# A two-layer decoder trunk: the mixer's gate projection in front of its key projection, and tile 1's output gate made by hand

## The chip, the cores and the metric

The kernel runs on one core of one Trainium2 chip. Its time is the device time of one execution in microseconds (us); lower is better. The engines are TensorE (PE, matrix products), VectorE (DVE), ScalarE (ACT), GpSimd (POOL) and SyncE (SP, which issues the transfers of the weights).

## The reference, cut to what matters

There are 256 tokens of width 1024 and two layers. Each layer is a half-step SwiGLU FFN, a token mixer and a second half-step FFN, each followed by a layer norm. The mixer is what the change touches:

```
h = x @ w_in                 # one projection, its columns split into groups
(nq, kc, vc, ks, vs, kw, vw, gl, u, gq, gk, gv, ga, gr) = split(h)
gates = sigmoid(gl)                                   # for the attention's three branches
o_a = nsa_mixer(nq, kc, vc, ks, vs, kw, vw, gates)    # compressed / selected / window attention
o_b = pool_mixer(u)                                   # trailing means
# gated linear attention:
log_a = log_sigmoid(ga @ wa2 + ba) / 16               # low-rank forget gate
b = cumsum(log_a) in chunks of 64;  q_t = gq * exp(b);  k_t = gk * exp(-b)
o_c = rmsnorm(gla(q_t, k_t, gv)) * norm_g * silu(gr)  # silu(gr) is the output gate
out = concat(o_a, o_b, o_c) @ w_out
```

In `nsa_mixer` the raw keys and values `kc`, `vc` are gathered into blocks of 32 positions, `pe` is added, and the blocks go through `gelu(flat @ w1) @ w2`: this is called the compression below.

## The kernel before, in words

**Tiles.** The 256 tokens are two tiles of 128, t = 0 and 1. The activations `x` are transposed on TensorE and kept as a high and a low part (`xh`, `xl`). A large matmul is three products of such parts (`mm3`): high by high, high by low, low by high.

**Weights.** A weight half (128x1024, or 128x592 for the gate chunk) is loaded by SP into one of four `raw` buffers. ACT copies its high part into `wh` (L236), VectorE makes the low part `wl = raw - wh` (L238); there are eight buffers of each. Both tiles use the same halves. The list `units` sets the order in which halves are loaded and split: FFN, then the mixer's projection in the order `WIN_ORDER`, four halves for each chunk, then the output projection, then the next FFN.

**The mixer's steps.** `ORDER` (L47) is the program order of the mixer, a letter for the step and a digit for the tile: `k` is `chunk_keys`, `g` `chunk_gates`, `f` `gates`, `q` `chunk_queries`, `c` `compress`, `v` `chunk_values`, `a` one step of the attention, `r` `chunk_rest` (the last chunk), `s` the load of ACT's silu table, `p` the pooling, `l` the end of the linear attention, `w` a step of the output projection. A scheduler then places instructions on the engines by priority along this order, as their inputs and buffers come, so the end of the FFN and its layer norm interleave with the first steps of the mixer. Each engine runs its instructions in the order so fixed.

- `chunk_keys` projects the keys and values. ACT copies them out of PSUM (`c0`, four key pieces; `kv`, the raw keys and values of the compression). TensorE transposes `c0`; ACT and VectorE make `ksh` and `ksl` of it. TensorE transposes `kv` into a bank of the kind `acc`; VectorE copies it with four `zr` copies and adds `pe` twice (`zA`, `zB`), 128x256 each.
- `chunk_gates` projects the gates. ACT copies `c3` (the attention's gates and the low-rank gate) and makes the silu of `gr` in `grs`. TensorE transposes `c3`, VectorE copies `gaT` (L604), TensorE multiplies it by `wa2` (L606), and ACT and VectorE begin the log-sigmoid (`az`, `mn`).
- `gates` loads ACT's table of exponential and logarithm (once, for tile 0), finishes the log-sigmoid, makes the cumulative sums `bc` by two scans and three exponentials of them (`eb`, `enb`, `ekh`), and `eg`, one plus an exponential of the attention's gates.
- `compress` needs `zA` and `zB` of both tiles: 32 matmuls on them (L676), a gelu on VectorE and ACT over the small tile `tg`, its copy `grep` (L691), and the product with `w2` (L694).
- `chunk_queries` copies the queries, transposes them, and keeps a high part on ACT (L762) and a correction on VectorE (L763), both in `qs`.
- `chunk_rest` projects the last chunk into `c4`, and GpSimd multiplies `grs` by `norm_g` (L772). That multiply is placed as soon as `grs` is there.
- The softmax of the attention is made by VectorE (scores with mask into `P`, L811) and ACT (exponential, L813); TensorE then transposes `P`.

PSUM has single banks `g0`, `g1`, `tr0`, `tr1`, and two banks each for `acc0` and `acc1`.

Of the kernel before, what the change touches and what calls it, by code (L numbers as in the profile page):

```python
# [10 lines left out]
def _warn_once_fixed(msg, *args, **kwargs):  # L11
# [11 lines left out]
AF = mybir.ActivationFunctionType  # L23
ALU = mybir.AluOpType
# [18 lines left out]

LAST = (10, 8, 9)
WARM = ((7, 512), (4, 128))
WIN_ORDER = (0, 3, 1, 2, 4)
ORDER = ("k0 g0 k1 g1 f0 f1 q0 c v0 a0 a0 a0 a0 q1 v1 a0 r1 a0 a1 a1 r0 a1 a1 a1 a1 a1 a1 a1 a1 s "  # L47
         "p0 l0 w0 w0 w0 p1 w0 w1 l1 w1 w0 w1 w1 w1")
TAGS = {
    "b2": (("c0", "c1", "qm"), 4),  # L50
    "b1": (("zr", "sq", "pl", "c2", "kv"), 3),
    "b05": (("c3", "az", "mn", "gaT", "qt", "kt", "kq"), 6),
    "P": (("P",), 4),
}
# [2 lines left out]
def build(ctx, tc, d):  # L57
    nc = tc.nc
    PE, ACT, DVE, POOL = nc.tensor, nc.scalar, nc.vector, nc.gpsimd
# [57 lines left out]
    for t in range(2):  # L117
        vbd.append(cst.tile([128, 2, 2, 64], F32, name=f"vbd{t}"))
        a = cst.tile([128, 4, 128], F32, name=f"at{t}")
# [57 lines left out]
    for l in range(L):  # L177
        def ffn_units(f):
            def down(c):
                if c >= 0:  # L180
                    halves([d["wd"][l, f, (2 * c + h) * 128:(2 * c + h + 1) * 128, :] for h in range(2)], 1024)

            for c, q in ((0, 0), (1, 0), (0, 1), (1, 1)) if (l, f) == (0, 0) else ((0, 0), (0, 1), (1, 0), (1, 1)):
                halves(gate_up(l, f, c, q), 1024)
            for x in PLAN:
                if x[0] == "S":
                    fs = seven(l, f, int(x[1:]))
                elif x[0] in "ab":
                    halves(gate_up(l, f, int(x[1:]), "ab".index(x[0])), 1024)
                elif x[0] == "d":  # L190
                    down(int(x[1:]))
                elif x[0] != "T":
                    units.append(fs[x])
            for c in LAST:
                down(c)
        ffn_units(0)
        for c in WIN_ORDER:
            for q in range(2):
# [92 lines left out]
    def bank(kind, t):  # L291

        return psum.tile([128, 512], F32, name=f"{kind}{t}", bufs=2 if kind == "acc" else 1)

    def transposes(t, srcs, kind="tr"):
        p = bank(kind, t)
        for i, s in enumerate(srcs):
            pe(PE.transpose(p[:, i * 128:(i + 1) * 128], s, ident))  # L298
        return p
# [274 lines left out]
    def mt(t, name, shape, dt=F32):  # L574
        for tag, (names, n) in TAGS.items():
            if name in names:
                return mix.tile(shape, dt, name=f"{name}{t}", tag=tag, bufs=n)
        return mix.tile(shape, dt, name=f"{name}{t}", bufs=1)

    def win_mm(m, t, n, kind):  # L580
        xh, xl = XT[t]
        ps = bank(kind, t)
        for q in range(2):
            u = unit(t)
            for h in range(2):
                wh, wl = u[h]
                for kk in range(2):
                    k = 4 * q + 2 * h + kk
                    s = slice(kk * n, kk * n + n)
                    mm3(ps[:, :n], xh[:, k, :], xl[:, k, :], wh[:, s], wl[:, s], k == 0, k == 7)  # L590
        return ps

    def chunk_gates(m, t):

        v, sm = m.t[t], m.sm
        ps = win_mm(m, t, W3, "g")
        grs = v["grs"] = mt(t, "grs", [128, 256])
        c3 = v["c3"] = mt(t, "c3", [128, 128])
        ACT.activation(out=c3, in_=ps[:, 168:296], func=AF.Copy)
        m.silu = ACT.activation(out=grs, in_=ps[:, 0:256], func=AF.Silu)  # L600

        p = transposes(t, [c3])
        gaT = mt(t, "gaT", [128, 128])
        DVE.tensor_copy(out=gaT, in_=p[:, 0:128])  # L604
        zp = bank("tr", t)
        PE.matmul(zp[:, 0:128], sm["wa2"], gaT, start=True, stop=True)  # L606
        az = v["az"] = mt(t, "az", [128, 128])
        mn = v["mn"] = mt(t, "mn", [128, 128])
        ba = sm["cols"][:, 0:1]
        ACT.activation(out=az, in_=zp[:, 0:128], func=AF.Abs, bias=ba)  # L610
        DVE.tensor_scalar(out=mn, in0=zp[:, 0:128], scalar1=ba, scalar2=0.0, op0=ALU.add, op1=ALU.min)

    def gates(m, t):

        v = m.t[t]
        az, mn = v["az"], v["mn"]
        if t == 0:
            with tc.issue_after(m.silu.ins):
                m.table = ACT.preload_act_table_set("natural_log_exp_and_others")

        eg = v["eg"] = mt(t, "eg", [128, 3, 4, 2])
        egf = eg.rearrange("p a b c -> p (a b c)")
        with tc.issue_after(m.table.ins):
            ACT.activation(out=az, in_=az, func=AF.Exp, scale=-1.0)
            ACT.activation(out=az, in_=az, func=AF.Ln, bias=1.0)
            ACT.activation(out=egf, in_=v["c3"][:, 104:128], func=AF.Exp, scale=-1.0)
        DVE.tensor_sub(out=mn, in0=mn, in1=az)
        bc = mt(t, "bc", [128, 128])
        for c in range(2):
            s = slice(c * 64, c * 64 + 64)  # L630
            DVE.tensor_tensor_scan(out=bc[:, s], data0=ones, data1=mn[:, s], initial=0.0, op0=ALU.mult, op1=ALU.add)
        bl = mt(t, "bl", [128, 2])
        DVE.tensor_scalar(out=bl, in0=bc[:, 63:128:64], scalar1=1.0 / 16, scalar2=None, op0=ALU.mult)
        eb = v["eb"] = mt(t, "eb", [128, 128])
        enb = v["enb"] = mt(t, "enb", [128, 128])
        ekh = v["ekh"] = mt(t, "ekh", [128, 128])
        ACT.activation(out=eb, in_=bc, func=AF.Exp, scale=1.0 / 16)
        ACT.activation(out=enb, in_=bc, func=AF.Exp, scale=-1.0 / 16)
        for c in range(2):
            s = slice(c * 64, c * 64 + 64)  # L640
            ACT.activation(out=ekh[:, s], in_=bc[:, s], func=AF.Exp, scale=-1.0 / 16, bias=bl[:, c:c + 1])
        DVE.tensor_scalar(out=egf, in0=egf, scalar1=1.0, scalar2=None, op0=ALU.add)

    def chunk_keys(m, t):

# [120 lines left out]
    def chunk_rest(m, t):  # L766

        v = m.t[t]
        ps = win_mm(m, t, 512, "g")
        c4 = v["c4"] = mt(t, "c4", [128, 512])  # L770
        ACT.activation(out=c4, in_=ps, func=AF.Copy)
        POOL.tensor_mul(out=v["grs"], in0=v["grs"], in1=m.sm["ng"])  # L772

    def cat_tiles(m, t):
        v = m.t[t]
# [179 lines left out]
    def wout(m, t):  # L955
        cth, ctl = cat_tiles(m, t)
        accs = [bank("acc", t), bank("acc", t)]
        for q in range(4):
            u = unit(t)
            order = [(kk, h) for kk in range(2) for h in range(2)]  # L960
            if q == 3:
                order.sort(key=lambda o: o[1])
            for kk, h in order:
                k = 2 * q + kk
                wh, wl = u[kk]
                s = slice(h * 512, h * 512 + 512)
                mm3(accs[h], cth[:, k, :], ctl[:, k, :], wh[:, s], wl[:, s], k == 0, k == 7)
            yield
        layer_norm(t, accs, m.l, 1)
        make_xT(t, sums=m.sums)  # L970


    def run(g, n=None):
        k = 0
        while n is None or k < n:
            if next(g, "end") == "end":
                return
            k += 1
# [54 lines left out]
    for l in range(L):  # L1033
        ffn(l, 0, sums, None)
        m = m0[0] if l == 0 else Mix(l)
        att = [attention(m, t) for t in range(2)]
        out = [wout(m, t) for t in range(2)]
        for op in ORDER.split():
            t = int(op[1]) if len(op) > 1 else 0
            if op == "c":  # L1040
                compress(m)
            elif op == "s":
                with tc.issue_after(m.last_exp.ins):
                    ACT.preload_act_table_set("silu_and_others")
            elif op[0] == "a":
                run(att[t], 1)
            elif op[0] == "w":
                run(out[t], 1)
            else:
                {"g": chunk_gates, "f": gates, "k": chunk_keys, "q": chunk_queries, "v": chunk_values, "r": chunk_rest, "p": pooling,  # L1050
                 "l": gla_out}[op[0]](m, t)
        for g in att + out:
            assert next(g, "end") == "end"
        nxt = {}
        ffn(l, 2, m.sums, nxt)
        sums = nxt
# [85 lines left out]
```

## Time and profile before

| what | value |
|---|---|
| median of 3 runs | 963.13 us (962.96 to 965.55) |
| the profiled execution | 964.65 us, its span 962.9 us |
| TensorE clock granted | 0.998 |
| busy: PE / DVE / ACT / POOL | 946.6 / 839.4 / 582.3 / 30.5 us |
| instructions in the span | 12738 |
| moved by DMA | 178.80 MB, mean 186 GB/s |
| mixer's projection, first layer | about 186.7 to 224 us of the span |
| the same, second layer | about 662.2 to 699.5 us |

The span runs from the first to the last instruction that the profiler shows; the execution's own time is 1.75 us longer. In a timeline row stand the start and the duration in us, the engine, the line, the operation, what it writes and reads with shapes, and in brackets how long the engine stood idle before it and whose result ended that. A matmul's record includes the time in which its result drains, so records of matmuls overlap.

### The profile page before, as it was taken

How to read it: one execution, taken by the hardware profiler on the slowest of the kernel's cores; microseconds unless marked ns; L12 is line 12 of the kernel's file. 1: busy time of each engine (PE TensorE's matmuls, PEld its weight loads, DVE VectorE, ACT ScalarE, POOL GpSimd, SP SyncE). 2: the span in 40 equal slices, each digit the busy share in tenths (PEclk: the TensorE clock that was granted, in tenths of full speed). 3: DMA queues.
4: the chain of work that ended last, by engine and by line, in shares of the span. 5: the costliest groups of instructions: out<-in, count | busy, mean ns of one | idle time of the engine just before them, and what ended most of it. 6: DMA issues, size and time to landing. Idle time of an engine off the chain costs nothing.

```text
span 962.9 us, 12738 instructions
## 1 busy us (share of the span) xinstructions
PE 946.6 (98%) x4563; PEld 776.1 (81%) x4563; DVE 839.4 (87%) x1244; ACT 582.3 (60%) x883; POOL 30.5 (3%) x48
## 2 busy tenths in 40 slices
PE   9999999999999999999999999999999999999996
PEld 6888888878778888888788888878777788888885
DVE  6999999887869988998899799988788699899985
ACT  6666666375755666766555666653777465666660
POOL 0000000010001000000000000001000010000000
PEclk9999999999999999999999999999999999999999
DMA  8764676564445555648673737474634474647341
GB/s 298 294 220 152 204 239 240 158 209 148 157 156 184 167 178 181 215 144 291 195 237 116 247 121 249 144 244 156 201 103 146 143 222 147 207 147 262 99 164 44
DMA packets 51872, 178.80 MB, mean 186 GB/s; under 512 B 6624, under 2 KB 7648, under 8 KB 51552
## 3 DMA queue, kind: packets, MB, share of 16 engines
q1 hardware_dynamic: 49824, 171.16, 53.2%
q0 software_dynamic: 1840, 6.75, 2.2%
q8 instruction: 36, 0.59, 0.3%
q14 instruction: 28, 0.23, 0.1%
q10 hardware_dynamic: 144, 0.07, 0.0%
HBM read 176.91 MB, written 1.05 MB: 185 GB/s over the span
## 4 chain that ended last, share of the span: by engine, by line
PE 91%; DVE 5%; DMA 2%; issue 1%; ACT 1%; SPq 0%; DVEq 0%; ACTq 0%
PE g L430 15%; PE acc L272 12%; PE acc L271 12%; PE acc L270 12%; PE tr L430 8%; PE g L272 5%; PE g L270 5%; PE g L271 5%; PE tr L272 3%; PE tr L271 3%; PE tr L270 3%; PE tr L298 2%; PE acc L289 1%; DMA raw<-in_wgu 1%; PE tr L505 1%; PE tr L289 1%
## 5 line engine op out<-in xcount | busy, mean ns | idle before, releaser
L238 DVE TENSOR_TENSOR wl<-raw,wh 128x1024 fp32r<-128x1024 f32 (+2 forms) x226 | 267.1, 1196 | 40.4 <-ACT wh L236 39.2
L236 ACT ACTIVATE wh<-raw 128x1024 fp32r<-128x1024 f32 (+2 forms) x226 | 232.2, 1038 | 110.2 <-PE acc L272 56.4
L216 ACT ACTIVATE wh<-fa 128x1024 fp32r<-128x1024 f32 x96 | 101.9, 1063 | 87.7 <-DVE fa L147 44.1
L270 PE MATMUL acc<-wh,hi 128*128 128x512 f32 x352 | 138.6, 394 | 0.2 <-ACT hi L275 0.2
L272 PE MATMUL acc<-wh,lo 128*128 128x512 f32 x352 | 137.4, 390 | 1.3 <-DVE lo L276 1.3
L271 PE MATMUL acc<-wl,hi 128*128 128x512 f32 x352 | 137.1, 389 | 0.0
L217 DVE TENSOR_TENSOR wl<-fa,wh 128x1024 fp32r<-128x1024 f32 x96 | 116.6, 1223 | 16.2 <-ACT wh L216 13.9
L270 PE MATMUL g<-wh,xh 128*128 128x512 f32 (+1 forms) x224 | 86.1, 384 | 0.0
L271 PE MATMUL g<-wl,xh 128*128 128x512 f32 (+1 forms) x224 | 85.7, 383 | 0.0
L272 PE MATMUL g<-wh,xl 128*128 128x512 f32 (+1 forms) x224 | 85.0, 379 | 0.0
L272 PEld LDWEIGHTS acc<-wh,lo 128*128 128x128 f32 x352 | 66.1, 188 | 16.1 <-DVE lo L276 2.4
L270 PEld LDWEIGHTS acc<-wh,hi 128*128 128x128 f32 x352 | 66.1, 188 | 14.1 <-ACT hi L275 1.0
L271 PEld LDWEIGHTS acc<-wl,hi 128*128 128x128 f32 x352 | 66.2, 188 | 13.3
L270 PE MATMUL acc<-wh,xh 128*128 128x512 f32 x128 | 51.2, 400 | 0.7 <-ACT wh L236 0.5
L271 PE MATMUL acc<-wl,xh 128*128 128x512 f32 x128 | 50.9, 398 | 0.2 <-DVE wl L238 0.2
L272 PE MATMUL acc<-wh,xl 128*128 128x512 f32 x128 | 50.4, 394 | 0.0
L270 PE MATMUL tr<-wh,xh 128*128 128x512 f32 x128 | 50.2, 392 | 0.0
L272 PE MATMUL tr<-wh,xl 128*128 128x512 f32 x128 | 49.9, 390 | 0.0
L271 PE MATMUL tr<-wl,xh 128*128 128x512 f32 x128 | 49.8, 389 | 0.0
L270 PEld LDWEIGHTS g<-wh,xh 128*128 128x128 f32 x224 | 42.1, 188 | 8.8 <-issue 1.6
L272 PEld LDWEIGHTS g<-wh,xl 128*128 128x128 f32 x224 | 42.1, 188 | 7.1
L271 PEld LDWEIGHTS g<-wl,xh 128*128 128x128 f32 x224 | 42.1, 188 | 7.1
(282 smaller groups left out, 1917.3 us busy)
## 6 DMA issues: line engine op xcount, KB each, us to landing
raw<-in_wgu SPq DMA_DIRECT2D x103, 512.0 KB, 4.1
raw<-in_wd SPq DMA_DIRECT2D x88, 512.0 KB, 4.7
raw<-in_win SPq DMA_DIRECT2D x32, 512.0 KB, 4.4
fa<-in_wgu SPq DMA_DIRECT2D x24, 512.0 KB, 4.5
fb<-in_wgu SPq DMA_DIRECT2D x24, 512.0 KB, 5.5
fc<-in_wgu SPq DMA_DIRECT2D x24, 512.0 KB, 5.0
raw<-in_wout SPq DMA_DIRECT2D x16, 512.0 KB, 3.7
lnp_ln_g<-in_ln_g POOLq DMA_DIRECT2D x5, 512.0 KB, 5.1
```

What stands on the lines that cost most here:

```text
L216: ACT.activation(out=wh[:, :w], in_=raw[:, :w], func=AF.Copy)
L217: DVE.tensor_sub(out=wl[:, :w], in0=raw[:, :w], in1=wh[:, :w].bitcast(F32))
L236: ACT.activation(out=wh[:, s], in_=raw[:, s], func=AF.Copy)
L238: DVE.tensor_sub(out=wl[:, s], in0=raw[:, s], in1=wh[:, s].bitcast(F32))
L270: pe(PE.matmul(ps, xh, wh, start=start, stop=False))
L271: pe(PE.matmul(ps, xh, wl, start=False, stop=False))
L272: pe(PE.matmul(ps, xl, wh, start=False, stop=stop))
L289: PE.matmul(out, lhsT, rhs, start=False, stop=True, skip_group_check=True)
L298: pe(PE.transpose(p[:, i * 128:(i + 1) * 128], s, ident))
L430: pe(PE.matmul(ps, a[:, k, :], w[:, s], start=first and k == 0 and n == 0, stop=k == 3 and n == 2, skip_group_check=True))
L505: pe(PE.transpose(p[:, i * 128:(i + 1) * 128], x, ident))
```

## The change

`WIN_ORDER` and `ORDER` put the gate chunk in front of the key chunk, for both tiles, in the loads and splits as in the program. The functions `chunk_gates` and `gates` become one (the body of `gates` follows at the end of `chunk_gates`), so a tile's whole gate arithmetic is placed with its gate projection; ACT's table is loaded right behind tile 0's silu. Tile 1's `gr` is copied raw, and its silu is made in `chunk_rest` of tile 1: exponential on ACT, plus one and reciprocal on VectorE, multiplication on GpSimd, ahead of the multiplication by `norm_g`. A buffer tag gets the name `gr`. The transposes of `kv` write a bank of the kind `acc` in both versions.

```diff
-WIN_ORDER = (0, 3, 1, 2, 4)
-ORDER = ("k0 g0 k1 g1 f0 f1 q0 c v0 a0 a0 a0 a0 q1 v1 a0 r1 a0 a1 a1 r0 a1 a1 a1 a1 a1 a1 a1 a1 s "
+WIN_ORDER = (3, 0, 1, 2, 4)
+ORDER = ("g0 k0 g1 k1 q0 c v0 a0 a0 a0 a0 q1 v1 a0 r1 a0 a1 a1 r0 a1 a1 a1 a1 a1 a1 a1 a1 s "
...
-    "b1": (("zr", "sq", "pl", "c2", "kv"), 3),
+    "b1": (("zr", "sq", "pl", "c2", "gr", "kv"), 3),
...
     def chunk_gates(m, t):
...
-        m.silu = ACT.activation(out=grs, in_=ps[:, 0:256], func=AF.Silu)
+        if t == 0:
+            silu = ACT.activation(out=grs, in_=ps[:, 0:256], func=AF.Silu)
+            with tc.issue_after(silu.ins):
+                m.table = ACT.preload_act_table_set("natural_log_exp_and_others")
+        else:
+            ACT.activation(out=grs, in_=ps[:, 0:256], func=AF.Copy)
+
+        eg = v["eg"] = mt(t, "eg", [128, 3, 4, 2])
+        egf = eg.rearrange("p a b c -> p (a b c)")
+        with tc.issue_after(m.table.ins):
+            ACT.activation(out=egf, in_=c3[:, 104:128], func=AF.Exp, scale=-1.0)
+        DVE.tensor_scalar(out=egf, in0=egf, scalar1=1.0, scalar2=None, op0=ALU.add)
...
-    def gates(m, t):
...
     def chunk_rest(m, t):
...
-        POOL.tensor_mul(out=v["grs"], in0=v["grs"], in1=m.sm["ng"])
+        grs = v["grs"]
+        if t == 1:
+
+            sg = mt(t, "gr", [128, 256])
+            ACT.activation(out=sg, in_=grs, func=AF.Exp, scale=-1.0)
+            DVE.tensor_scalar(out=sg, in0=sg, scalar1=1.0, scalar2=None, op0=ALU.add)
+            DVE.reciprocal(out=sg, in_=sg)
+            POOL.tensor_mul(out=grs, in0=grs, in1=sg)
+        POOL.tensor_mul(out=grs, in0=grs, in1=m.sm["ng"])
```

Where the instructions stand now, at three places of the first layer. The rows give the line, the operation, what is written and read, and the shape; numbers tell buffers of one name apart.

TensorE, tile 1's gates: from the transposition of `c3` (named `c_1938` and `c_1911`) to the product with `wa2`. Before:

```order
L298 MATMUL tr_1941<-ident,c_1938 128x128
L270 MATMUL g_1988<-wh,xh_1651 128x512
L271 MATMUL g_1988<-wl,xh_1651 128x512
L272 MATMUL g_1988<-wh,xl_1652 128x512
L270 MATMUL g_1988<-wh,xh_1651 128x512
L606 MATMUL tr_1945<-gaT_1943,s_wa_1192 128x128
```

After, the end of the same stretch (the transposition `L298 MATMUL tr_1917<-ident,c_1911 128x128` stands ahead of it, with five more of these matmuls between):

```order
L271 MATMUL acc_1942<-wl,xh_1717 128x512
L272 MATMUL acc_1942<-wh,xl_1718 128x512
L270 MATMUL acc_1942<-wh,xh_1717 128x512
L271 MATMUL acc_1942<-wl,xh_1717 128x512
L272 MATMUL acc_1942<-wh,xl_1718 128x512
L270 MATMUL acc_1942<-wh,xh_1717 128x512
L617 MATMUL tr_1921<-gaT_1919,s_wa_1192 128x128
```

Between the two stood four matmuls of tile 0's queries (`g_1988`); now eleven of tile 1's keys (`acc_1942`).

VectorE, tile 1's keys and gates up to the compression. Before, `zA`, `zB` and `gaT` of tile 1 come ahead of the gate arithmetic of both tiles:

```order
L276 TENSOR_TENSOR ksl<-tr_1895,ksh 128x4x128
L665 COPY zr_1905<-acc_1902 64x2x8x8
L238 TENSOR_TENSOR wl<-raw,wh 128x1024
L667 TENSOR_TENSOR zA<-zr_1905,s_pe 128x8x32
L667 TENSOR_TENSOR zB<-zr_1905,s_pe 128x8x32
L604 COPY gaT_1943<-tr_1941 128x128
L238 TENSOR_TENSOR wl<-raw,wh 128x1024
L611 TENSOR_SCALAR mn_1948<-tr_1945,s_cols 128x128
L627 TENSOR_TENSOR mn_1863<-mn_1863,az_1862 128x128
```

After, they come behind it, with two weight splits between them and the query corrections:

```order
L238 TENSOR_TENSOR wl<-raw,wh 128x1024
L629 SCALAR_TENSOR_TENSOR bc_1930<-ones,mn_1924 128x64 x2
L662 COPY zr_1981<-acc_1978 64x2x8x8
L631 TENSOR_SCALAR bl_1933<-bc_1930 128x2
L276 TENSOR_TENSOR ksl<-tr_1971,ksh 128x4x128
L662 COPY zr_1981<-acc_1978 64x2x8x8 x3
L238 TENSOR_TENSOR wl<-raw,wh 128x1024
L664 TENSOR_TENSOR zA<-zr_1981,s_pe 128x8x32
L664 TENSOR_TENSOR zB<-zr_1981,s_pe 128x8x32
L238 TENSOR_TENSOR wl<-raw,wh 128x1024 x2
L760 SCALAR_TENSOR_TENSOR qs_2037<-tr_2040,qs_2037 64x512
```

The pair `zA`, `zB` of tile 1 moved from ahead of its gates to the end of the row of work in front of the compression.

VectorE, the compression's gelu. Before, both query corrections (`qs`) stand inside it:

```order
L680 COPY xg<-tr_2056 64x30 x2
L763 SCALAR_TENSOR_TENSOR qs_2037<-tr_2040,qs_2037 64x512
L683 TENSOR_TENSOR tg<-xg 128x30
L684 SCALAR_TENSOR_TENSOR tg<-tg,xg 128x30
L686 SCALAR_TENSOR_TENSOR tg<-tg,xg 128x30
L688 TENSOR_SCALAR tg<-tg 128x30
L689 RECIPROCAL tg<-tg 128x30
L690 TENSOR_TENSOR tg<-tg,xg 128x30
L763 SCALAR_TENSOR_TENSOR qs_2037<-tr_2049,qs_2037 64x512
L691 COPY grep<-tg 128x8x15
```

After:

```order
L760 SCALAR_TENSOR_TENSOR qs_2037<-tr_2040,qs_2037 64x512
L677 COPY xg<-tr_2056 64x30 x2
L680 TENSOR_TENSOR tg<-xg 128x30
L681 SCALAR_TENSOR_TENSOR tg<-tg,xg 128x30
L683 SCALAR_TENSOR_TENSOR tg<-tg,xg 128x30
L760 SCALAR_TENSOR_TENSOR qs_2037<-tr_2049,qs_2037 64x512
L685 TENSOR_SCALAR tg<-tg 128x30
L686 RECIPROCAL tg<-tg 128x30
L687 TENSOR_TENSOR tg<-tg,xg 128x30
L688 COPY grep<-tg 128x8x15
```

The first correction moved ahead of the gelu, the second to the place where the gelu's exponential is made on ACT.

Elsewhere: on VectorE, tile 1's +1 (L774) and reciprocal (L775) stand ahead of the last two weight splits in front of tile 1's softmax; on ACT, its exponential (L773) stands ahead of the last two of its splits there. On POOL, tile 0's multiply by `norm_g` now stands between the two layer-norm steps (L365) of the first FFN, tile 1's two multiplies behind the loads of four constants of the next layer. In the second layer, the first two halves that are loaded while the first FFN ends are of the gate chunk.

More of the change, by code (lines that the diff above doesn't have):

```diff
@@ L597, in chunk_gates @@
         grs = v["grs"] = mt(t, "grs", [128, 256])
-        c3 = v["c3"] = mt(t, "c3", [128, 128])
+        c3 = mt(t, "c3", [128, 128])
         ACT.activation(out=c3, in_=ps[:, 168:296], func=AF.Copy)
-        m.silu = ACT.activation(out=grs, in_=ps[:, 0:256], func=AF.Silu)
+        if t == 0:
[9 more added lines that the diff above has]
+        DVE.tensor_scalar(out=egf, in0=egf, scalar1=1.0, scalar2=None, op0=ALU.add)
         p = transposes(t, [c3])
@@ L606, in chunk_gates @@
         PE.matmul(zp[:, 0:128], sm["wa2"], gaT, start=True, stop=True)
-        az = v["az"] = mt(t, "az", [128, 128])
-        mn = v["mn"] = mt(t, "mn", [128, 128])
+        az = mt(t, "az", [128, 128])
+        mn = mt(t, "mn", [128, 128])
         ba = sm["cols"][:, 0:1]
@@ L611, in chunk_gates @@
         DVE.tensor_scalar(out=mn, in0=zp[:, 0:128], scalar1=ba, scalar2=0.0, op0=ALU.add, op1=ALU.min)
-    def gates(m, t):
[L615 to L626, printed above, removed]
+        ACT.activation(out=az, in_=az, func=AF.Exp, scale=-1.0)
+        ACT.activation(out=az, in_=az, func=AF.Ln, bias=1.0)
         DVE.tensor_sub(out=mn, in0=mn, in1=az)
@@ L641, in gates @@
             ACT.activation(out=ekh[:, s], in_=bc[:, s], func=AF.Exp, scale=-1.0 / 16, bias=bl[:, c:c + 1])
-        DVE.tensor_scalar(out=egf, in0=egf, scalar1=1.0, scalar2=None, op0=ALU.add)
     def chunk_keys(m, t):
@@ L1049, in build @@
             else:
-                {"g": chunk_gates, "f": gates, "k": chunk_keys, "q": chunk_queries, "v": chunk_values, "r": chunk_rest, "p": pooling,
+                {"g": chunk_gates, "k": chunk_keys, "q": chunk_queries, "v": chunk_values, "r": chunk_rest, "p": pooling,
                  "l": gla_out}[op[0]](m, t)
```

## The prediction

> **What bounds the kernel now.** I read the page's head and its chain of waits first, to see which engine sets the end; then TensorE's own waits, which must be few where TensorE is nearly always busy; then the timeline around each of them, to see what came late; and last the stretches in which the changed instructions will run.
>
> ```profile
> span 962.9 us, 12738 instructions
> PE 946.6 (98%) x4563; PEld 776.1 (81%) x4563; DVE 839.4 (87%) x1244; ACT 582.3 (60%) x883; POOL 30.5 (3%) x48
> PE 91%; DVE 5%; DMA 2%; issue 1%; ACT 1%; SPq 0%; DVEq 0%; ACTq 0%
> ```
>
> TensorE (PE) is the bound: 946.6 of 962.9 us, so all its gaps together are 16.3 us and no reordering can give more. No matmul is added or taken away. The question is only which gaps close and which open. In the first layer's mixer (stretch 180 to 240) TensorE's waits are these three:
>
> ```profile
> PE tr L606 <- DVE gaT L604: 1.8, 2, 1.1
> PE tr L694 <- DVE grep L691: 0.6, 1, 0.6
> ```
>
> Their places, from TensorE's timeline, with the first key matmul, the first gate matmul, the first query matmul of tile 0 and the start of the compression:
>
> ```profile
> 186.66 0.39 PE L270 MATMUL acc<-wh,xh 128*128 128x512 f32 x1
> ...
> 192.10 0.29 PE L270 MATMUL g<-wh,xh 128*128 128x296 f32 x1
> 192.23 0.30 PE L271 MATMUL g<-wl,xh 128*128 128x296 f32 x1
> ...
> 198.39 0.40 PE L272 MATMUL acc<-wh,xl 128*128 128x512 f32 x1
> 199.56 0.49 PE L606 MATMUL tr<-gaT,s_wa 128*128 128x128 f32 x2 [0.77 <-DVE gaT L604]
> ...
> 208.03 0.40 PE L270 MATMUL g<-wh,xh 128*128 128x512 f32 x1
> ...
> 209.54 0.39 PE L270 MATMUL g<-wh,xh 128*128 128x512 f32 x1
> 211.00 0.49 PE L606 MATMUL tr<-gaT,s_wa 128*128 128x128 f32 x2 [1.07 <-DVE gaT L604]
> ...
> 215.20 0.67 PE L676 MATMUL tr<-zA,s_w 128*128 128x60 f32 x5
> ...
> 222.38 0.40 PE L270 MATMUL acc<-wh,xh 128*128 128x512 f32 x1
> 223.41 0.46 PE L694 MATMUL tr<-grep,s_w2k 128*128 128x128 f32 x2 [0.64 <-DVE grep L691]
> ```
>
> A record includes the drain of a matmul, so I count from start to start: a 512-wide one takes (192.10 - 186.66) / 24 = 0.227 us, a 296-wide one about 0.13. Over these steps the gaps lose 199.56 - 198.39 - 0.23 = 0.94, 211.00 - 209.54 - 0.23 = 1.23 and 223.41 - 222.38 - 0.23 = 0.80 us: 2.97 in all, 2.17 of it ahead of the compression. The second layer has the same three, and one of its own where its first FFN ends, which starts with the split of the first weights of the projection (ACT makes `wh`, VectorE `wl`):
>
> ```profile
> 644.73 1.06 ACT L236 ACTIVATE wh<-raw 128x1024 fp32r<-128x1024 f32 x1 [0.98 <-DMA raw<-in_win]
> ...
> 645.82 1.23 DVE L238 TENSOR_TENSOR wl<-raw,wh 128x1024 fp32r<-128x1024 f32 x1 [0.82 <-ACT wh L236]
> 646.96 1.28 DVE L276 TENSOR_TENSOR lo<-tr,hi 128x512 fp32r<-128x512 f32 x2
> ...
> 646.66 0.40 PE L271 MATMUL acc<-wl,hi 128*128 128x512 f32 x1
> 647.70 0.50 PE L272 MATMUL acc<-wh,lo 128*128 128x512 f32 x1 [0.65 <-DVE lo L276]
> ```
>
> The transfer is late, ACT's split behind it, VectorE's split behind that, and the `lo` that TensorE needs last of all: 647.70 - 646.66 - 0.23 = 0.81, and about 0.1 just ahead of it, 0.9 in all.
>
> **The change, part by part.** *Second layer's FFN end.* The halves that arrive here become 592 wide instead of 1024. What a 592-wide split takes on ACT and on VectorE:
>
> ```profile
> 188.48 0.70 ACT L236 ACTIVATE wh<-raw 128x592 fp32r<-128x592 f32 x1 [1.60 <-DMA raw<-in_win]
> 190.06 0.72 DVE L238 TENSOR_TENSOR wl<-raw,wh 128x592 fp32r<-128x592 f32 x1
> ```
>
> Against the 1.06 and 1.23 above each split is 0.4 to 0.5 shorter, and 42% less is transferred before it; a proportionate arrival puts both splits in ahead of the need at 646.66 + 0.23 = 646.9. The gain lies between 0.4 (only the shorter splits) and 0.9; I take 0.9, since the transfers are what the rows above wait for.
>
> *Gates ahead of keys.* The 24 gate matmuls of a tile now run first. For tile 0 eight key matmuls (1.8 us) stand between the gate transposition and the product at the old L606, for tile 1 eleven (2.5 us), where four stood (0.9). What VectorE has to do meanwhile decides. Its rows before, with GpSimd's (POOL) beside them:
>
> ```profile
> 195.70 0.68 DVE L276 TENSOR_TENSOR ksl<-tr,ksh 128x512 fp32r<-128x512 f32 x1
> 196.30 1.61 DVE L665 COPY zr<-acc 64x128 f32<-64x128 f32 x4
> 197.94 0.91 DVE L667 TENSOR_TENSOR zA<-zr,s_pe 128x256 f32<-128x256 f32 x1
> 198.77 0.41 DVE L667 TENSOR_TENSOR zB<-zr,s_pe 128x256 f32<-128x256 f32 x1
> 199.22 0.29 DVE L604 COPY gaT<-tr 128x128 f32<-128x128 f32 x1
> 199.92 1.23 DVE L238 TENSOR_TENSOR wl<-raw,wh 128x1024 fp32r<-128x1024 f32 x1 [0.41 <-ACT wh L236]
> ...
> 208.18 1.23 DVE L238 TENSOR_TENSOR wl<-raw,wh 128x1024 fp32r<-128x1024 f32 x1
> 209.32 0.96 DVE L667 TENSOR_TENSOR zA<-zr,s_pe 128x256 f32<-128x256 f32 x1
> ...
> 197.83 0.73 POOL L772 TENSOR_TENSOR grs<-grs,s_ng 128x256 f32<-128x256 f32 x1 [3.48 <-ACT grs L600]
> ...
> 208.93 1.07 POOL L772 TENSOR_TENSOR grs<-grs,s_ng 128x256 f32<-128x256 f32 x1 [10.37 <-ACT grs L600]
> ```
>
> `gaT` came late because a key pass of 0.6 (ksl), four `zr` copies, `zA` and `zB` stood ahead of it. In the new order tile 0's `gaT` has none of them ahead, so the 0.94 goes. Tile 1's has ksl, `zr` and two weight splits ahead, and eleven matmuls as cover: I leave 0.4 of its wait. Three other TensorE steps now wait for ACT, because key copies follow its 1024-wide splits (about 1 us each): 0.1 at tile 0's `c3`, 0.2 at tile 1's, 0.25 at tile 1's key copy. These four are estimates from adding up the new rows of ACT and VectorE by the steps above; their ends are 0 and, one 1024-wide split late at three places, about 3 us. TensorE without any wait would reach the compression at 215.20 - 2.17 = 213.03; with 0.95 it is 213.98.
>
> VectorE must be done with tile 1's `zA` and `zB` by then, and these are now the last of its queue, where only tile 0's query matmuls (24 x 0.227 = 5.4 us) cover them. Its first 1024-wide split after the layer norm stands at 199.92 before; by the new order of ACT, which makes that weight half right after tile 0's gate exponentials, I put it at 199.6. From there it has six of them at 209.32 - 208.18 = 1.14 (6.84), two ksl at 0.60 (1.20), eight `zr` at 0.40 (3.2), two `zA` and `zB`, and gate pieces worth some 1.2. With four passes at 0.42 it ends at 199.6 + 6.84 + 1.2 + 3.2 + 1.7 + 1.2 = 213.8, level with TensorE. With the `zA` of before (0.83 to the next start) it ends at 214.6.
>
> Which `zA` holds? `zA` and `zB` are the same operation on the same shape, 0.91 and 0.41. Both `zA` run beside a GpSimd multiply, no `zB` does. After the change neither `zA` has one beside it: tile 0's multiply is issued in the layer norm, tile 1's with the last chunk. So I take 0.41 for it, and 214.1 for the compression, between 213.98 and 214.6 and near the first. Gain 1.1 per layer.
>
> The Trainium skill, "SBUF — State Buffer", section "SBUF: two separate sides", says that VectorE and GpSimd share one port pair as an exclusive lock, and that a VectorE operation with two SBUF inputs and a GpSimd operation cannot run at once. The 0.91 against 0.41 agrees with that. By this rule the sum is as I have it here, while without it (a `zA` that is slow for a reason of its own) the compression starts at 214.6 and each layer gains 0.6 instead of 1.1. The same rule speaks against the change at one place, tile 1's two multiplies, which then stand beside weight splits.
>
> *Compression's activation.* Out of its VectorE chain, the step behind ACT's exponential, the second query correction and the end:
>
> ```profile
> 221.39 0.18 DVE L688 TENSOR_SCALAR tg<-tg 128x30 f32<-128x30 f32 x1 [0.29 <-ACT tg L687]
> ...
> 222.21 0.69 DVE L763 SCALAR_TENSOR_TENSOR qs<-tr,qs 64x512 fp32r<-64x512 f32 x1
> 222.93 0.23 DVE L691 COPY grep<-tg 128x120 f32<-128x120 f32 x1
> ```
>
> Two query corrections (`qs`, 222.93 - 222.21 = 0.72 each) stand inside the chain to `grep`. Now the first is ahead of the chain and the second stands where VectorE waits for ACT's exponential (0.29 of idle time before), so `grep` comes up to 1.44 - 0.43 = 1.0 earlier. ACT makes its second query copy ahead of the exponential now, which can take some 0.5 of that back. Of the 0.80 I count 0.55 as gone; ends 0.3 and 0.8.
>
> *The output gate of tile 1 by hand.* Per layer this adds an exponential on ACT, two VectorE passes and a GpSimd multiply. They fall around VectorE's idle time ahead of tile 1's first softmax pass:
>
> ```profile
> 251.65 1.22 DVE L238 TENSOR_TENSOR wl<-raw,wh 128x1024 fp32r<-128x1024 f32 x1
> 255.71 0.42 DVE L811 CUSTOM_DVE_ANT_0 P<-acc,cau 128x256 f32<-128x256 f32 x1 [2.84 <-PE acc L289]
> ...
> 221.61 0.34 DVE L689 RECIPROCAL tg<-tg 128x30 f32<-128x30 f32 x1
> ...
> 257.88 0.16 DVE L816 RECIPROCAL cf<-cf 128x2 f32<-128x2 f32 x1
> ```
>
> The reciprocal of 128x256 has no row. From 30 and 2 elements, (0.34 - 0.16) / 28 = 6.5 ns for each, so about 1.8 us; the +1 is like `zB`, 0.41. Ends: 0.41 (a plain pass) and 2.5. Two weight splits are queued behind the reciprocal, and the softmax behind them: 2.2 of the 2.84 idle are used. If the two multiplies hold VectorE up as they held `zA`, 2 x 0.5, the softmax starts some 0.4 late, and part of that TensorE has other matmuls for. I count 0.15 per layer, ends 0 and 1.0. ACT, 60% busy, has room for an exponential of 0.4. Moving the table load (1.3) to tile 0's gates puts it where ACT waits for the layer norm; the DMA issues on POOL that now stand behind the multiplies bring constants that the next layer needs hundreds of microseconds later; SP's queue changes only the order of eight halves. All at nothing. The keys' transpositions use the two `acc` banks in both versions.
>
> **Sum.** 2 x 1.1 + 2 x 0.55 + 0.9 - 2 x 0.15 = 3.9 us. The profiled execution took 964.65, so 960.75 on that base; 1.5 above the median of the three runs. Against the median of 963.13 the forecast is 959.2.
>
> **The rivals.** *All gaps close:* 2 x 2.97 + 0.9 = 6.8 gives 956.3. For it speaks that every matmul gap has more cover than before; against it that ACT's splits stand in between. *The waits only move:* tile 1's gate product, its key copy and `zA` take back what the first gap gave, and what is left is the FFN end and the activation, 0.9 + 1.1: 961.1, or with the activation unchanged 962.2. For it: VectorE's queue ends level with TensorE's arrival, without reserve. That the change does no part of what it says for the keys' bank falls in here. *Slower:* tile 1's `zB` is 4.6 us ready ahead of the compression before (210.2 + 0.4 against 215.20) and has no reserve after. Each microsecond by which VectorE's queue starts late costs one in each layer. From 1.4 late plus the other gains, (0.9 + 2 x 0.4) / 2 = 0.85, so 2.25, the change loses; 4 late gives 2 x (4 - 2.25) = 3.5 slower, 966.6. Against it: ACT is 60% busy, and needs three splits late in a row to do that.
>
> **How the numbers follow.** A difference under 0.3%, 2.9 us, cannot be told from none here: the bounds are 960.2 and 966.0. The forecast has 0.52 (own range 957.7 to 960.4), all gaps 0.11, moved waits 0.30, slower 0.07. The range from 956.6 to 962.6 leaves out the slower case, and the edges of the other two. Faster: 0.48 of the forecast, 0.11, and a few of the moved waits, 0.62; same 0.31; slower 0.07.
>
> **What would show it.** In the changed profile the wait for `gaT` should be under 0.5 in sum per layer, `zA` about 0.41, the second layer's wait for `lo` gone, the compression 1.1 earlier after the FFN's end. TensorE waiting for `zA` or `zB` at the compression, or for `c`, shows the moved waits; a softmax of tile 1 that starts late after the reciprocal shows the price of the gate by hand. A reciprocal well over 2.5 us, or a layer norm that ends over 1 us later because of the 1024-wide splits in it, would make me wrong.

## The result, and the profile after

The changed kernel takes 958.22 us (median of 5 runs, 957.58 to 958.43) against 963.2 (5 runs, 962.96 to 965.55): the ratio is 0.9935, 95% interval 0.9922 to 0.9949. It is 5.0 us faster, where 959.2 was forecast. The page of its profiled execution (958.23 us) begins:

```profile
span 956.5 us, 12750 instructions
PE 945.7 (99%) x4563; PEld 775.9 (81%) x4563; DVE 841.2 (88%) x1248; ACT 582.6 (61%) x885; POOL 36.2 (4%) x50
```

TensorE does the same work (945.7 against 946.6 us busy), so the time came out of its gaps. These are its waits for VectorE in the whole run:

```profile
PE acc L106 <- DVE zw L109: 1.2, 1, 1.2
PE tr L617 <- DVE gaT L615: 0.7, 2, 0.3
PE acc L272 <- DVE lo L276: 0.5, 1, 0.5
```

In the whole run before, three of them were:

```profile
PE tr L606 <- DVE gaT L604: 3.7, 4, 1.1
PE acc L272 <- DVE lo L276: 1.3, 2, 0.7
PE tr L694 <- DVE grep L691: 1.2, 2, 0.6
```

Of the four waits for `gaT` two are left, and shorter; the wait for `grep` is gone from the list; the remaining wait for `lo` is at 464.40, in the first layer's second FFN, where the change does nothing. In the timeline of the first mixer:

```profile
186.02 0.29 PE L270 MATMUL g<-wh,xh 128*128 128x296 f32 x1
...
203.20 0.39 PE L270 MATMUL acc<-wh,xh 128*128 128x512 f32 x1
203.93 0.49 PE L617 MATMUL tr<-gaT,s_wa 128*128 128x128 f32 x2 [0.34 <-DVE gaT L615]
...
212.95 1.67 PE L673 MATMUL tr<-zA,s_w 128*128 128x60 f32 x14
...
220.15 0.39 PE L270 MATMUL acc<-wh,xh 128*128 128x512 f32 x1
220.68 0.46 PE L691 MATMUL tr<-grep,s_w2k 128*128 128x128 f32 x2
```

From the first matmul of the mixer to the compression it took 215.20 - 186.66 = 28.54 us, and now 212.95 - 186.02 = 26.93. Start to start, the gaps that are left lose 203.93 - 203.20 - 0.23 = 0.50 and 220.68 - 220.15 - 0.23 = 0.30.

The two profiles' spans differ by 6.4, which is 1.4 more than the medians. To keep that apart, I measure each layer's mixer on TensorE, from its first projection matmul to the first large FFN product behind it: before 336.69 - 186.66 = 150.03 and 812.06 - 662.18 = 149.88, after 334.03 - 186.02 = 148.01 and 805.65 - 657.77 = 147.88. The last part of the second layer's first FFN (from its first product with `hi` to the mixer) took 662.18 - 603.09 = 59.09 and takes 657.77 - 599.84 = 57.93. In all four kernels here that load the keys first it takes 59.1 to 59.8, in those that load the gates first 57.9 to 58.0 (58.4 in one), so this gap is closed by the order of the halves. Together this is 2.0 + 2.0 + 1.2 = 5.2. The rest of the 6.4 is 0.6 ahead of the first mixer and 0.6 in the first layer's second FFN; both stretches vary by as much between runs of kernels that do not differ there.

### The profile page after: what moved, and what is told of

It is laid out like the page before. It is cut to its first block, busy times and chain, and to the rows that moved or that the text cites. A ratio compares the mean times of both kernels' runs of the same rounds, so it can differ in the third digit from the quotient of the medians.

```text
span 956.5 us, 12750 instructions
## 1 busy us (share of the span) xinstructions
PE 945.7 (99%) x4563; PEld 775.9 (81%) x4563; DVE 841.2 (88%) x1248; ACT 582.6 (61%) x885; POOL 36.2 (4%) x50
## 4 chain that ended last, share of the span: by engine, by line
PE 95%; DVE 2%; DMA 1%; ACT 1%; issue 0%; DVEq 0%; ACTq 0%
PE g L430 15%; PE acc L272 12%; PE acc L270 12%; PE acc L271 12%; PE tr L430 8%; PE g L270 5%; PE g L271 5%; PE g L272 5%; PE tr L272 3%; PE tr L271 3%; PE tr L270 3%; PE tr L298 3%; PE acc L289 1%; PE tr L505 1%; PE tr L289 1%; PE g L505 1%
```

## The experiments

**One part alone: the order of the chunks.** Edit of the kernel before:

```diff
-WIN_ORDER = (0, 3, 1, 2, 4)
-ORDER = ("k0 g0 k1 g1 f0 f1 q0 c v0 ...
+WIN_ORDER = (3, 0, 1, 2, 4)
+ORDER = ("g0 k0 g1 k1 f0 f1 q0 c v0 ...
```

> The kernel before with only the two orders changed: gate chunk ahead of key chunk for both tiles, in the loads and in the program; both output gates still made by ScalarE's silu, the exponential table still loaded behind tile 1's silu, the rest of the gate arithmetic still after both tiles. Theory (the place of the gate chunk is what gives the time, because gaT no longer stands behind ksl, zr, zA and zB): the second layer's 0.9 at the FFN's end, some 0.5 per layer at grep, tile 0's 0.94 per layer and at least half of tile 1's 1.23 per layer: 4.0 to 5.0 us faster, 958.2 to 959.2. Rival (the merged gate arithmetic and the silu by hand are needed, since the table load and both tiles' exponentials otherwise hold up ScalarE's splits): 1 to 2 us faster, 961 to 962, with waits of TensorE for keys or zA ahead of the compression.

Measured: 959.75 us against 963.64 for before on the same chip, ratio 0.9962 (0.9949 to 0.9974), 3.9 us faster. The theory was right on its main point and a little high: the changed kernel is still about 1.3 faster (the mixers take 148.72 and 148.63 here, 0.7 more each). Where that is, TensorE's and VectorE's timelines show:

```profile
213.00 0.39 PE L272 MATMUL g<-wh,xl 128*128 128x512 f32 x1
213.97 0.74 PE L676 MATMUL tr<-zA,s_w 128*128 128x60 f32 x5 [0.58 <-PE g L272]
...
213.44 0.42 DVE L667 TENSOR_TENSOR zA<-zr,s_pe 128x256 f32<-128x256 f32 x1
```

The bracket names a matmul that had long started; what ended 0.1 ahead of the compression is `zA` (213.44 + 0.42). VectorE's queue ends about 0.7 too late here, with both tiles' gate arithmetic in its last part and one weight split more: five stand between the two tiles' `zA`, where the changed kernel has four. This is the "waits only move" rival, in small.

**The other part alone: merged gates, early table, silu by hand.** Edit of the changed kernel: the two orders put back, with `k0 g0 k1 g1 q0 c`.

> The changed kernel with the two orders put back (keys ahead of gates): merged gate arithmetic, early table load and tile 1's silu by hand stay. Theory: gaT still stands behind zr, zA and zB on VectorE, so the waits at its product stay near 0.9 (tile 0) and fall to 0.7 (tile 1, whose multiply on GpSimd is gone from beside zA) and the second layer's FFN end keeps its 0.9: 0 to 1.5 us faster than before, 961.7 to 963.2. Rival: half or more of the gain, below 960.7.

Measured: 962.41, ratio 0.999 (0.9981 to 0.9999), 1.2 faster than before: as the theory said. Two views of it, the waits and VectorE's timeline:

```profile
PE tr L617 <- DVE gaT L615: 1.5, 2, 0.8
PE tr L298 <- DVE ksl L276: 1.3, 2, 0.6
```
```profile
197.67 0.91 DVE L664 TENSOR_TENSOR zA<-zr,s_pe 128x256 f32<-128x256 f32 x1
...
209.02 0.41 DVE L664 TENSOR_TENSOR zA<-zr,s_pe 128x256 f32<-128x256 f32 x1
```

Tile 0 still waits for `gaT` by 0.77, tile 1 does so no more, but its transposition of `c3` waits for `ksl` instead. And in one kernel there are now both kinds of `zA`: tile 0's beside GpSimd's multiply, 0.91, and tile 1's without, 0.41. The mixers take 149.57 and 149.35, 0.5 less each, which is about what tile 1's `zA` lost (0.96 - 0.41); that the merged arithmetic or the early table gives anything beyond this is not shown. The two parts add up: 3.9 + 1.2 = 5.1, against 5.0 for the whole, though each has an interval of about 1 us to either side.

**What makes `zA` slow.** The kernel before, with the multiplies meant to be later:

```diff
-        ACT.activation(out=c4, in_=ps, func=AF.Copy)
-        POOL.tensor_mul(out=v["grs"], in0=v["grs"], in1=m.sm["ng"])
+        c4i = ACT.activation(out=c4, in_=ps, func=AF.Copy)
+        with tc.issue_after(c4i.ins):
+            POOL.tensor_mul(out=v["grs"], in0=v["grs"], in1=m.sm["ng"])
```

> The kernel before, with GpSimd's two multiplies by norm_g issued behind the copy of the last chunk instead of as soon as grs is there; nothing else moves. Theory (zA takes 0.91 instead of 0.41 only because a GpSimd multiply runs beside it, and gaT stands behind zA): all four zA take 0.41, each of the four waits for gaT falls by 0.5: 2.0 us faster, 961.2. Rival (zA is slow for a reason of its own): zA stays at 0.9 and the time at 963.2.

Measured: 963.39, ratio 1.0 (0.9991 to 1.0009), and `zA` at 0.91 to 0.97. But the edit did not do what it was for. GpSimd's timeline:

```profile
197.21 0.73 POOL L773 TENSOR_TENSOR grs<-grs,s_ng 128x256 f32<-128x256 f32 x1 [3.48 <-ACT grs L600]
```

As the bracket shows, the multiply still waits for nothing but `grs`: `issue_after` gave an order to the planner (the scheduler that fixes each engine's sequence) and no wait for the last chunk. So the run tells nothing of the rival. The second try puts a GpSimd operation in front that really reads the last chunk:

```diff
+        pin = mt(t, "pin", [128, 1])
+        p1 = POOL.tensor_mul(out=pin, in0=c4[:, 0:1], in1=c4[:, 0:1])
+        with tc.issue_after(p1.ins):
+            POOL.tensor_mul(out=v["grs"], in0=v["grs"], in1=m.sm["ng"])
```

> The kernel before, with GpSimd's two multiplies by norm_g held back for certain: a one-column GpSimd multiply that reads the last chunk's copy is queued in front of each. The run late_mult had the same aim, and there the multiplies stayed at 197 and 208 us beside zA. Theory (a GpSimd multiply at the same time makes zA take 0.91 instead of 0.41, and gaT stands behind zA): all four zA take 0.41, the four waits for gaT fall by 0.4 to 0.5 each: 1.6 to 2.0 us faster than before, about 961.6. Rival (zA is slow for a reason of its own): zA stays at 0.9, no change from before.

Measured: 961.62 against 963.83, ratio 0.9981 (0.9972 to 0.999): 2.2 us faster from moving two GpSimd multiplies in each layer. Its `zA` group, its waits for `gaT`, and the first multiply where it stands now:

```profile
L667 DVE TENSOR_TENSOR zA<-zr,s_pe x4: 418/422/425, 197.5 to 682.0; 128x256 f32<-128x256 f32 x4
```
```profile
PE tr L606 <- DVE gaT L604: 1.1, 3, 0.5
```
```profile
253.77 0.73 POOL L775 TENSOR_TENSOR grs<-grs,s_ng 128x256 f32<-128x256 f32 x1
```

All four `zA` take 0.42, and the waits for `gaT` fell from 3.7 to 1.1 (one of them became a wait of 0.6 for `c3`). The mixers take 149.06 and 148.84, 1.0 less each. So the overlap with a GpSimd multiply is what doubles `zA`; the next run shows it the other way round. It also means that about half of the 2.0 that the change gains in a mixer could be had in the old order, by moving these multiplies alone.

**The same cost put into the changed kernel.** A GpSimd multiply beside each `zA`:

```diff
+        scr = mt(t, "scr", [128, 256])
+        zf = zr.rearrange("p a i k -> p (a i k)")
+        POOL.tensor_mul(out=scr, in0=zf, in1=zf)
         for ab, z in ((0, m.zA), (1, m.zB)):
```

> The changed kernel with a GpSimd multiply of zr by itself into a spare tile added right behind the zr copies of either tile, so that it runs beside zA. Theory of the shared access: zA grows from 0.42 to 0.8 to 0.95 at all four places. What it costs: by the prediction's reckoning 0.5 per layer (959.3); the rival reckoning, from the changed kernel's rows: tile 1's zA ends at 212.48 and TensorE takes it at 212.95, and gaT stands ahead of zA now, so the time stays at 958.2 to 958.6.

Measured: 959.26, ratio to before 0.9954 (0.9942 to 0.9966). Tile 1, GpSimd's, VectorE's and TensorE's rows:

```profile
212.37 1.64 POOL L665 TENSOR_TENSOR scr<-zr 128x256 f32<-128x256 f32 x1 [5.76 <-DVE zr L662]
...
213.46 0.84 DVE L667 TENSOR_TENSOR zA<-zr,s_pe 128x256 f32<-128x256 f32 x1
...
213.97 0.39 PE L272 MATMUL g<-wh,xl 128*128 128x512 f32 x1
214.39 0.85 PE L676 MATMUL tr<-zA,s_w 128*128 128x60 f32 x6
```

Tile 1's `zA` doubles to 0.84, tile 0's only grows to 0.53, since there the GpSimd operation starts early. The compression starts 0.42 after the matmul in front of it, 0.2 late. The mixers take 148.28 and 148.18, 0.3 more each. Neither expectation held exactly: the cost lies between none and the prediction's 0.5 per layer. The 959.26 alone would fit the expected 959.3, but it lies only 1.0 and 0.8 above the changed kernel's 958.22 and 958.48, which are from other sets of runs; the mixers are the better measure. In the new order, with `gaT` ahead of `zA`, the same overlap costs less than the 1.0 per mixer that two multiplies cost before.

**Tile 1's silu by hand.** Left out: its exponential, plus one, reciprocal and multiply.

```diff
-            sg = mt(t, "gr", [128, 256])
-            ACT.activation(out=sg, in_=grs, func=AF.Exp, scale=-1.0)
-            DVE.tensor_scalar(out=sg, in0=sg, scalar1=1.0, scalar2=None, op0=ALU.add)
-            DVE.reciprocal(out=sg, in_=sg)
-            POOL.tensor_mul(out=grs, in0=grs, in1=sg)
```

> The changed kernel without tile 1's silu: its exponential, plus one, reciprocal and the multiply by the result are left out (grs stays the raw gate times norm_g); everything else as in the changed kernel. Theory (the gate by hand lies in VectorE's idle time ahead of tile 1's softmax): the same time, 958.2 within 0.4. Rival (it holds the softmax up by 0.2 to 0.5 per layer): 957.2 to 957.8.

Measured: 958.48 (957.85 to 958.9), mixers 148.02 and 147.90: the same as with it, to 0.1 per mixer. It is free. How near that is to not being free, VectorE's and GpSimd's timelines of the changed kernel show:

```profile
247.16 0.28 DVE L774 TENSOR_SCALAR gr<-gr 128x256 f32<-128x256 f32 x1
247.54 0.78 DVE L729 COPY_PREDICATED at<-glam,tr 128x256 f32<-128x256 uint8 x2
248.21 1.74 DVE L775 RECIPROCAL gr<-gr 128x256 f32<-128x256 f32 x1
249.88 2.83 DVE L238 TENSOR_TENSOR wl<-raw,wh 128x1024 fp32r<-128x1024 f32 x2
253.03 0.42 DVE L816 CUSTOM_DVE_ANT_0 P<-acc,cau 128x256 f32<-128x256 f32 x1 [0.33 <-PE acc L289]
...
250.10 1.52 POOL L776 TENSOR_TENSOR grs<-grs,gr 128x256 f32<-128x256 f32 x1 [27.18 <-DVE gr L775]
251.70 1.60 POOL L777 TENSOR_TENSOR grs<-grs,s_ng 128x256 f32<-128x256 f32 x1
```

Of the idle 2.84 us in front of the softmax 0.33 is left.

**That cover taken away.** The reciprocal three times in a row (and, in the other run, twice):

```diff
-            DVE.reciprocal(out=sg, in_=sg)
+            for _ in range(3):
+                DVE.reciprocal(out=sg, in_=sg)
```

> The changed kernel with the reciprocal of tile 1's gate made three times in a row (the value is the same): 3.5 us more on VectorE in each layer, ahead of tile 1's softmax, where 0.33 us of idle time is left. Theory (the softmax's start sets TensorE there, with a reserve under 1 us): the softmax starts 3.1 later and each layer loses 2.2 to 3.1: 962.6 to 964.4. Rival (TensorE has other matmuls for that time): under 1 us per layer, below 960.3.

> The changed kernel with tile 1's reciprocal made twice, so that its output gate is wrong (the reciprocal of the reciprocal): 1.74 us more on VectorE per layer, where 0.33 is left before the softmax. recip3 (3.5 us more) lost 5 to 6 us per layer, part of it because the planner moved TensorE's work as well. Theory (every microsecond beyond the idle time is paid, and more behind it): 1.4 to 3 us per layer, 961 to 964. Rival (TensorE's reserve covers the first 1.7 us): within 0.5 of after_rep.

Measured: three times, 968.9 (ratio to before 1.0051, 1.0038 to 1.0064); twice, 963.09 (0.9996, 0.9987 to 1.0004) beside 958.48 for the changed kernel on the same chip. So the run with 1.74 us more on VectorE is 4.6 slower in all, 2.5 per mixer (150.57 and 150.42), inside the expectation; the one with 3.5 more is some 10 slower, 6.1 and 5.0 per mixer (154.13, 152.86), and there the expectation was far too low. VectorE's last split and tile 1's softmax in the run with two:

```profile
252.90 1.16 DVE L238 TENSOR_TENSOR wl<-raw,wh 128x1024 fp32r<-128x1024 f32 x1
253.97 0.41 DVE L817 CUSTOM_DVE_ANT_0 P<-acc,cau 128x256 f32<-128x256 f32 x1
```

From the mixer's start the softmax begins at 253.97 - 186.24 = 67.73, against 253.03 - 186.02 = 67.01 in the changed kernel. That is 0.7 later and not the 1.74 - 0.33 = 1.4 that the expectation counts, in part because the two splits in front of it take 1.16 each and no longer 2.83 together: GpSimd's multiplies come later now. So the number fell inside the expectation, but the softmax's start alone is 0.7 of the 2.5. The waits stand far behind the reciprocal; the first row is of the run with two, the second of that with three:

```profile
274.74 0.66 PE L298 MATMUL tr<-ident,P 128*128 128x128 f32 x4 [1.25 <-ACT pT L866]
```
```profile
289.97 0.41 PE L298 MATMUL tr<-ident,sq 128*128 128x128 f32 x2 [1.03 <-DVE sq L927]
```

With the longer queue the planner also puts TensorE's work in another order (transposes of `P` behind more projection matmuls), so how much of the rest is VectorE's delay and how much the order stays open. What is shown is that the idle time is used up and the softmax starts late; what each microsecond of that costs is not.

**The wait that is left.** `gaT` of tile 1 stands behind ksl and four `zr` copies. In the first edit it gets ahead of them, in the second ScalarE makes it:

```diff
+        with tc.high_priority():
             DVE.tensor_copy(out=gaT, in_=p[:, 0:128])
```
```diff
-        DVE.tensor_copy(out=gaT, in_=p[:, 0:128])
+        ACT.activation(out=gaT, in_=p[:, 0:128], func=AF.Copy)
```

> The changed kernel with gaT's copy at high priority: VectorE makes tile 1's gaT ahead of ksl and the four zr copies, and the product with wa2 is placed four matmuls behind the transposition instead of eleven. Theory: the two waits of 0.5 that are left at that product go: 957.3. Rival (the copy then waits for the transposition itself, or ksl and zr come late for the compression): no change, 958.2 or above.

> The changed kernel itself once more, as the measure for the other runs of this call: 958.2 within 0.5.

> The kernel of hp_gat once more beside the changed kernel on the same chip, since its two waits for gaT were gone and its time came out at 957.98. From the profiles the mixers (first gate matmul to the first large FFN product behind) take 147.77 against 148.01 and 147.62 against 147.88: theory 0.5 faster than after_rep; rival (the early copy only delays ksl and zr): no difference.

> The changed kernel with gaT copied by ScalarE instead of VectorE, right behind tile 1's eg on its queue and ahead of the next weight splits. Theory: the waits for gaT go as in hp_gat and VectorE has 0.2 less to do per tile: 957.6. Rival (ScalarE then waits for the transposition with two weight splits behind it, and the compression gets late): 958.5 or more.

Measured: with high priority 957.98 in the first set of runs (ratio to before 0.9947, 0.9935 to 0.9959), in which the changed kernel was not. In the second, on one chip, 957.31 (957.04 to 957.62) beside 958.48 (957.69 to 959.37) for the changed kernel; the ratios to before are 0.9934 (0.9921 to 0.9946) and 0.9946 (0.9933 to 0.9958). It is the fastest kernel here, by about 1 us, though the two intervals overlap. Its mixers, 147.78 and 147.58, are 0.3 shorter than those of the changed kernel in that set (148.14 and 147.83). That is 0.6, and only this can be put down to `gaT`. The profiled executions (957.62 and 959.37) differ by 1.2 more: 0.7 ahead of the first mixer, which starts at 186.23 and 186.97, and 0.4 in the first layer's second FFN. The edit does nothing there, and the changed kernel's own two profiles differ by 1.0 in the first of these (186.02 and 186.97). The timeline with high priority has `gaT` right behind a weight split, and the product without a wait:

```profile
201.37 0.28 DVE L616 COPY gaT<-tr 128x128 f32<-128x128 f32 x1
...
201.84 0.38 PE L618 MATMUL tr<-gaT,s_wa 128*128 128x128 f32 x2
```

With ScalarE's copy 959.58 (0.996, 0.9946 to 0.9973), 1.1 slower than the changed kernel, with mixers of 148.78 and 148.67; the rival held in its number. The waits for `gaT` are gone there too, but:

```profile
212.78 0.39 PE L272 MATMUL g<-wh,xl 128*128 128x512 f32 x1
214.05 1.74 PE L673 MATMUL tr<-zA,s_w 128*128 128x60 f32 x14 [0.88 <-PE g L272]
...
213.53 0.42 DVE L664 TENSOR_TENSOR zA<-zr,s_pe 128x256 f32<-128x256 f32 x1
```

The planner put five weight splits between the two tiles' `zA` on VectorE, one more than in the changed kernel, so tile 1's `zA` ends at 213.95, and the compression waits 1.0 for it in each layer: a wait that moved and grew. Why the planner did so is not shown; with high priority the gate arithmetic stands as early, and there are four. The rival's own reason, ScalarE held up at the copy, is not in the trace: ScalarE makes `gaT` at 201.56 and goes on to the next split at 201.74.

## Why the prediction was right, point by point

- **The bound and the three gaps.** Right: the time came from TensorE's gaps at `gaT`, `grep` and the second layer's `lo`.
- **The second layer's FFN end** (0.9 taken, ends 0.4 and 0.9). Right in its way, a little small: 59.09 - 57.93 = 1.2. The new rows on ACT and VectorE, with no wait behind them at TensorE:

```profile
639.77 0.70 ACT L236 ACTIVATE wh<-raw 128x592 fp32r<-128x592 f32 x1 [0.16 <-DMA raw<-in_win]
...
639.06 2.60 DVE L238 TENSOR_TENSOR wl<-raw,wh 128x1024 fp32r<-128x1024 f32 x3 [0.51 <-ACT wh L236]
641.57 1.28 DVE L276 TENSOR_TENSOR lo<-tr,hi 128x512 fp32r<-128x512 f32 x2
```

- **Gates ahead of keys** (1.1 per layer taken). The mechanism was right, the size too small: 28.54 - 26.93 = 1.6. The four new waits were put at 0.95 in all; only tile 1's `gaT` is there, with 0.50 (0.4 forecast). The three for ACT (0.1, 0.2, 0.25) are in no list of waits; start to start the places lose under 0.1 each. That is the term that was most mis-sized: 0.5 per layer, as much as the 1.0 us by which the forecast of 959.2 is above the measured 958.22.
- **VectorE's queue and `zA`.** Predicted from its first 1024-wide split to the end 213.8 - 199.6 = 14.2 us; its rows give

```profile
198.85 2.36 DVE L238 TENSOR_TENSOR wl<-raw,wh 128x1024 fp32r<-128x1024 f32 x2 [1.80 <-ACT wh L236]
...
212.06 0.42 DVE L664 TENSOR_TENSOR zA<-zr,s_pe 128x256 f32<-128x256 f32 x1
212.40 0.42 DVE L664 TENSOR_TENSOR zB<-zr,s_pe 128x256 f32<-128x256 f32 x1
```

  212.40 + 0.42 - 198.85 = 14.0, and `zA` is at 0.42. What the reckoning missed: the compression needs only `zA` when it starts, and `zB` 16 matmuls later, so `zB` did not belong into the end of the queue. `zA` ends at 212.48, TensorE comes at 212.95. The reserve is under 0.5, less than one weight split takes, and the two runs with one split more in front of it lost it.
- **Compression's activation** (0.55 taken). 8.21 us from the start of the compression to the product with `w2` became 7.73: 0.48, near enough. What ACT's second query copy takes back, put at some 0.5, is there too: VectorE waits 0.54 for it inside the chain.

```profile
218.02 0.60 ACT L759 ACTIVATE qs<-tr 128x512 fp32r<-128x512 f32 x1 [2.32 <-PE tr L298]
...
218.66 0.69 DVE L760 SCALAR_TENSOR_TENSOR qs<-tr,qs 64x512 fp32r<-64x512 f32 x1 [0.54 <-ACT qs L759]
```

- **The gate by hand** (0.15 per layer taken, ends 0 and 1.0). It costs 0, by the run without it. The reciprocal was estimated at 1.8 and takes 1.74; the plus one takes 0.28 and not 0.41; the two multiplies cost the weight splits 2.83 - 2.36 = 0.47 and not 1.0.
- **The sum.** With the measured terms it is 2 x 1.6 + 2 x 0.5 + 1.2 - 0 = 5.4, against 5.2 by the stretches of the two profiles and 5.0 by the medians. Three of the four terms erred the same way, towards too small a gain, so the forecast is not near by errors that cancel; where the last 0.2 to 0.4 went is not shown.
- **The rivals.** "The waits only move" was not what happened here, but the runs show it one step away: a copy on another engine turned 0.5 at `gaT` into 1.0 at the compression, per layer. The one on the slower side needed VectorE's queue 2.25 us late; it was on time.

## What to carry to other kernels

Where one engine is busy 98%, list its gaps and look for what stands in the late engine's queue in front of the operation that it waits for; a change of order among independent chunks can close the gap without any work saved. Then look at what becomes last in that queue: a small change of one copy can move the wait to the next consumer and make it larger. Work put into an idle stretch is free only while the idle time lasts, so read how much is left: here 0.33 us. The kernel with 1.74 more there lost 2.5 per layer, but its softmax began only 0.7 late and TensorE's work stood in another order, so compare the orders before you put a loss down to the added work.

## What the runs showed of the hardware

A VectorE addition of 128x256 takes 0.42 us alone and 0.84 to 0.97 beside a GpSimd multiply of the same size (0.53 where the multiply ends early in it). The multiply suffers too: 0.73 us where it starts first, as beside tile 0's `zA` in the kernel before, and 1.52 to 1.64 where it starts just behind a weight split. The Trainium skill, "SBUF — State Buffer", section "SBUF: two separate sides", states that the two engines share a port pair as an exclusive lock when a VectorE operation has two SBUF inputs and GpSimd reads SBUF; the runs with the multiplies moved away and put back agree.

The rows also look like one operation that stands still until the other is done, and not like two at half speed. In the kernel before, `zA` ends 0.29 and 0.28 behind the end of the multiply beside it (198.56 and 198.85, 210.00 and 210.28), and 0.29 behind it with the multiply put back (214.01 and 214.30), whatever their lengths. And the weight split at 212.31 of that last run, in which the multiply of 212.37 starts, takes 1.23 as it does alone; it is the multiply that grows, to 1.64.

The doubling was in the prediction; that GpSimd's side suffers was not, nor that four multiplies of an engine that is 3% busy, moved some 45 to 65 us later, would alone be worth 2.2 us in the kernel before. Their place decided it: they fell beside the operation in front of the one that TensorE waited for.
